# Softplus in place of bound, Exp and Ln in the first attention layer of a two-layer decoder, with a new instruction order

## The chip, the cores and the metric

The kernel runs on one core of one Trainium2 chip. The metric is device time in microseconds (us), from one launch. PE is the matmul engine, PEld its weight loads, DVE the vector engine, ACT the engine that evaluates functions and evacuates accumulators, POOL a general engine that cannot read the accumulators (PSUM), and SP issues nearly all transfers.

## The reference

2048 tokens of width 1024 get 16 meta tokens ahead of them. Two layers follow, each as norm, projection, attention, gate, output projection, residual; then a last norm.

```python
# layer 0: two groups of 8 heads
z = q @ k * 64**-0.5                              # stick-breaking heads
log_beta = log_sigmoid(z)
log_1m = where(s < t, log_beta - z, 0)            # = -softplus(z)
a = where(s < t, exp(log_beta + suffix_sum(log_1m)), 0);  o_sb = a @ v
p = softmax(where(s <= t, qk * 96**-0.5, -1e30)); o_mla = p @ v   # latent heads
h += concat(o_sb * silu(g_sb), o_mla * silu(g_mla)) @ w_out
# layer 1: 16 heads on a window of 128 keys, 16 meta keys, a sink logit, ALiBi
h += (attention(h) * silu(g)) @ w_out
out = rmsnorm(h)[:, meta dropped]
```

Since log_beta + suffix is z minus the sum of softplus over this key and all later keys, `a` is the exponential of one number for each key and query.

## The kernel before, in words

The sequence is cut into 17 blocks of 122 positions. Matmuls of the projections, of the scores and of the sums over keys take 32-bit operands that are rounded to a shorter format (`fp32r`), each split into a high and a low part, so that one product is three matmuls. The products with values (`av`, `mav`) are done in full 32 bit.

The stages, in order: norm, transposition and value projection (to about 100 us); the latent vectors and the other projections of layer 0, with the row maxima of the latent heads (to about 720 us); attention of layer 0 (to about 1645 us); output projection, norm and transposition, `out_mm`, `scale`, `turn`, `place` (to about 1865 us); the projections of layer 1; then attention of layer 1, in units of four heads of one block of 108 queries, between whose matmuls the kernel puts first the matmuls of the gates (`gates`, to about 2380 us) and then those of the last output projection (`project`, `final`, to the end).

**Layer 0 attention.** Heads go in 4 pairs, queries in 5 groups of up to 4 blocks (488 columns). For each pair and group a loop runs over key blocks. One step of the loop does, for both heads of the pair:

- `qks` (PE): scores of the stick-breaking head into `zp` (PSUM), 2 matmuls. Row 0 of each key block is an extra row that carries the running sum from key block to key block.
- `z` (DVE): `zcl` bounds the scores at 44 in place; on the diagonal it takes the minimum with a table `mz` that also holds the mask.
- `e`, `l` (ACT): `sp` = Exp of `zp`, then Ln(1 + `sp`) in place; together a softplus.
- `c` (DVE): `carry` writes row 0 of `sp` from row 0 of the step before.
- `h`, `lo`: high part (a cast, DVE) and low part (a difference, POOL, or DVE if the plan moves it) of `sp`.
- `tri` (PE): 2 matmuls with a triangle of -1 add the sums into `zp`; `a` (ACT): Exp of `zp`; `avs` (PE): product with the values.
- `qkm` (PE, 3 matmuls, a mask matmul on the diagonal), `p` (ACT: Exp), `acc` (POOL: sum of `p`), `avm` (PE) for the latent head.

At the end of a group `dn` (PE) makes the denominators, `rd` (ACT) their reciprocals as Ln and then Exp(-x), `rm` (POOL) multiplies, and `og` goes to DRAM. The values of the stick-breaking heads are stored doubled, because row 0 of the first step gives ln 2 to each sum.

The order of these instructions on each engine is fixed ahead of time: `attention_plan` lists the operations with costs and dependencies, `list_schedule` places them by a priority (`RANK`), by the sizes of the buffer rings (`RINGS`; `zp` has 2 per head) and by rules on when an operation may move to its second engine (`MOVE`). Engines then run that order and wait on semaphores.

**Functions on ACT.** ACT holds one table of functions at a time. The first instruction of the kernel loads the table `natural_log_exp_and_others`, which has Exp and Ln; Copy and Square are used with any table. Besides attention 0, Ln and Exp stand in `rstd` (L390 Ln, L391 Exp: one reciprocal root of the mean square; 17 blocks after attention 0, 16 of the last norm) and in `gate_evac` (L1662 Exp, L1663 Ln, L1664 Exp: the gate's sigmoid, 40 pieces). The softmax of layer 1 is Exp alone (L1576).

In layer 1 the units follow each other in one written order: `scores(x)` on PE and its maxima on DVE, `scale(x-1)` on DVE and POOL, filler matmuls, `trans(x-2)` on PE with its copies `ptsb` on ACT (L1598) and DVE, `exps(x)` on ACT, filler matmuls, `attend(x-3)`. A gate's three ACT operations are put in at the next filler but one after its matmuls.

Of the kernel before, what the change touches and what calls it, by code (L numbers as in the profile page):

```python
# [45 lines left out]
def constants():  # L46
# [15 lines left out]
    me = np.full((P, GW), ZMAX, f)  # L62
    me[1:BC, :BK] = np.where(i[:, None] < i[None, :], ZMAX, NEG)
    c["mz"] = me
    c["mk"], c["mk0"] = mk, mk0
# [58 lines left out]
def attention_plan():  # L124
# [31 lines left out]
    def act(n):  # L156
        return n / 1.4 + 196

    def gps(n):
        return n * 2.1 + 148  # L160

    groups = [(p, g) for p in range(NPAIR) for g in (4, 3, 2, 1, 0)]
    qk_s = qk_m = None
    q_ends, done, i = [], {}, 0
    for gi, (p, g) in enumerate(groups):
# [9 lines left out]
        for t in range(G.b1):  # L175
# [12 lines left out]
            for m in range(2):  # L188
                b_zp, b_a, b_sp, b_h, b_l = (buf(f"{x}{m}") for x in ("zp", "a", "sp", "h", "l"))
                qk_s = op("qks", s, m, "PE", pe(2, s.ns), [qk_s], [b_zp], late=late_s)  # L190
                o = op("z", s, m, "DVE", dve(s.ns) + 60, [qk_s])
                o = op("e", s, m, "ACT", act(s.ns) - 40, [o], [b_sp])
                o = op("l", s, m, "ACT", act(s.ns), [o])
                if prev:
                    o = op("c", s, m, "DVE", dve(prev.ns), [o, tri[m]], rel=[b_tri[m]])
                o = op("h", s, m, "DVE", dve(s.ns), [o], [b_h], alt=("ACT", act(s.ns)))
                o = op("lo", s, m, "Pool", gps(s.ns), [o], [b_l], [b_sp], alt=("DVE", 2 * dve(s.ns)))
                o = tri[m] = op("tri", s, m, "PE", pe(2, s.ns), [o], rel=[b_h, b_l])
                b_tri[m] = b_zp
# [38 lines left out]
RINGS = dict(zp0=2, zp1=2, a0=2, a1=2, sp0=2, sp1=2, h0=2, h1=2, l0=2, l1=2, av=1, mav=1, ms=2,  # L238
             p0=2, p1=2, acc0=3, acc1=3)
RANK = dict(qks=-8.69, z=-2.85, e=2.79, l=-3.38, c=0.83, h=6.8, lo=-5.92, tri=-1.18, a=3.58, avs=1.76, ogs=-0.44, qkm=-1.61, p=3.19, acc=8.47, avm=1.59, ogm=7.44, dn=1.64, rd=-5.97, rm=-9.39, head=0.74, other=-3.4)  # L240
MOVE = dict(lo=922, acc=1386, h=1245)
HEAD = {("lo", "tri"): -200, ("a", "avs"): -40, ("p", "avm"): -40}
CROSS = dict(PE=220, ACT=190, DVE=150, Pool=130)
OWN = dict(ACT=140, DVE=60, Pool=120, PE=0)


def list_schedule(ops, rank=RANK, move=MOVE, rings=RINGS):

    engines = ("PE", "ACT", "DVE", "Pool")
    free = dict(rings)  # L250
    users, wait, rt, pri = {}, {}, {}, {}
# [10 lines left out]
    while len(out) < len(ops):  # L262
        again = True
        while again:
            again = False
            for e in engines:
# [3 lines left out]
                for src in engines:  # L270
                    for o in ready[src]:
                        own = src == e
                        if rt[o] > now or not own and (not o.alt or o.alt[0] != e or busy[src] - now < move[o.kind]):
                            continue
                        if any(free[b.ring] <= 0 for b in o.acq):
                            continue
                        k = (pri[o][0] + (0 if own else rank["other"]), pri[o][1])
                        if best is None or k < best[0]:
                            best = (k, o, src)
                if best:  # L280
                    _, o, src = best
                    ready[src].remove(o)
                    for b in o.acq:
                        free[b.ring] -= 1
                    o.on, o.start = e, now
                    busy[e] = now + (o.cost if src == e else o.alt[1])
                    tick += 1
                    heapq.heappush(events, (busy[e], tick, "end", o))
                    out.append(o)
                    again = True  # L290
        if not events:
            break
        while True:
            now, _, what, x = heapq.heappop(events)
            if what == "end":
                for y, w in x.outs:
                    wait[y] -= 1
                    rt[y] = max(rt[y], now + w + (CROSS if y.eng != x.on else OWN)[x.on])
                    if wait[y] == 0:
# [3 lines left out]
                for b in x.rel:  # L303
                    users[b] -= 1
                    if users[b] == 0:
                        tick += 1
                        heapq.heappush(events, (now + CROSS[x.on], tick, "free", b))
# [11 lines left out]
def build(tc, a, off, upto=99):  # L319
# [121 lines left out]
    def open_b2():  # L441
# [6 lines left out]
        dma(cp, a["pack"][:, p0:p1])  # L448
        for n in ("ident", "tri", "mk", "mk0"):
# [72 lines left out]
    with ExitStack() as st:  # L522
# [20 lines left out]
        with ExitStack() as st2:  # L543
# [442 lines left out]
    with b2:  # L986
# [21 lines left out]
        def qks(s, m):  # L1008
# [5 lines left out]
            T.matmul(zp[:BC, :s.ns], k[:, 2 * m, c], q, start=True, stop=False)  # L1014
            T.matmul(zp[:BC, :s.ns], k[:, 2 * m + 1, c], q, start=False, stop=True)  # L1015

        def on_(e):
            return V if e == "DVE" else G

        def zcl(s, m):  # L1020

            z = s.zp[m][:BC, :s.ns]
            if s.bs >= s.G.b0:
                V.tensor_tensor(z, z, C("mz")[:BC, :s.ns], op=ALU.min)
            else:
                V.tensor_scalar(z, z, ZMAX, None, op0=ALU.min)  # L1026

        def exp1(s, m):
            sp = s.sp[m] = work(f"sp{m}", 2)
            S.activation(sp[:BC, :s.ns], s.zp[m][:BC, :s.ns], AF.Exp)  # L1030

        def log1(s, m):
            sp = s.sp[m][:BC, :s.ns]
            S.activation(sp, sp, AF.Ln, bias=1.0)  # L1034

        def carry(s, m):

            n, k = s.ns, s.prev.ns
            V.tensor_scalar(s.sp[m][0:1, n - k:n], s.prev.zp[m][0:1, :k], -1.0, None, op0=ALU.mult)  # L1039

# [19 lines left out]
        def aexp(s, m):  # L1060
            x = s.a[m] = work(f"a{m}", 2)
            S.activation(x[:BC, :s.ns], s.zp[m][:BC, :s.ns], AF.Exp)  # L1062

# [66 lines left out]
        def rden(s, m):  # L1130
            g, n = s.G, s.G.n
            r = g.r = work("rd", 1)
            S.activation(r[:, :n], g.dn[:, :n], AF.Ln)
            S.activation(r[:, :n], r[:, :n], AF.Exp, scale=-1.0)

        def rmul(s, m):
# [746 lines left out]
```

## Time and profile before

| | us |
|---|---|
| median of 3 runs (lowest, highest) | 2658.41 (2655.79, 2659.16) |
| the profiled execution, its own device time | 2655.23 |
| its span, first to last instruction | 2653.3 |
| PE busy in the span | 2605.3 (98%) |
| DVE, ACT, POOL busy | 1680.3, 1348.5, 1113.2 |
| layer 0 attention, 723 to 1645 us | 922 |
| gates beside layer 1 attention, 2096 to 2380 us | 284 |

Busy is the time in which an engine executes. PE's matmuls overlap, and their ends in the trace are modelled, so that a busy PE may still be one that waits; the start of one matmul to the start of the next is the safer measure. The trace's columns "idle before, releaser" say what ended an engine's wait. The profiled execution is 3.18 us below the median of the runs.

### The profile page before, as it was taken

How to read it: one execution, taken by the hardware profiler on the slowest of the kernel's cores; microseconds unless marked ns; L12 is line 12 of the kernel's file. 1: busy time of each engine (PE TensorE's matmuls, PEld its weight loads, DVE VectorE, ACT ScalarE, POOL GpSimd, SP SyncE). 2: the span in 40 equal slices, each digit the busy share in tenths (PEclk: the TensorE clock that was granted, in tenths of full speed). 3: DMA queues.
4: the chain of work that ended last, by engine and by line, in shares of the span. 5: the costliest groups of instructions: out<-in, count | busy, mean ns of one | idle time of the engine just before them, and what ended most of it. 6: DMA issues, size and time to landing. Idle time of an engine off the chain costs nothing.

```text
span 2653.3 us, 39563 instructions
## 1 busy us (share of the span) xinstructions
PE 2605.3 (98%) x13241; PEld 1961.4 (74%) x13241; DVE 1680.3 (63%) x3699; ACT 1348.5 (51%) x3311; POOL 1113.2 (42%) x938
## 2 busy tenths in 40 slices
PE   9999999999989999999999999999999999999998
PEld 7888888998945555555555555788999988777776
DVE  5366486777267767767776776433322478897884
ACT  6542121212267777777777776332222477764442
POOL 1012210010078878878877887410000123446552
PEclk9999999999999999999999999999999999999999
DMA  5476634342593351252232112643644545677652
GB/s 148 105 217 175 187 105 117 87 113 75 149 188 82 77 147 50 66 130 48 69 86 77 35 35 75 187 121 92 164 115 123 129 122 138 160 185 220 180 169 98
DMA packets 337862, 321.53 MB, mean 121 GB/s; under 512 B 143670, under 2 KB 319610, under 8 KB 337075
## 3 DMA queue, kind: packets, MB, share of 16 engines
q1 hardware_dynamic: 336939, 318.12, 44.9%
q8 instruction: 104, 1.70, 0.3%
q14 instruction: 99, 0.81, 0.1%
q10 hardware_dynamic: 720, 0.89, 0.1%
HBM read 198.46 MB, written 120.80 MB: 120 GB/s over the span
## 4 chain that ended last, share of the span: by engine, by line
PE 88%; DVE 4%; DMA 2%; ACT 2%; issue 1%; SPq 1%; POOL 1%; DVEq 0%; POOLq 0%; ACTq 0%
PE psd L397 8%; PE psd L398 8%; PE psd L399 8%; PE pso L1758 7%; PE psg L1645 6%; PE mav L1116 5%; PE av L1070 5%; PE zp L1014 4%; PE zp L1057 3%; PE psx L934 3%; PE zp L1058 3%; PE zp L1015 2%; PE pso L1238 2%; PE pso L1236 2%; PE pso L1237 2%; PE ms L1090 2%
## 5 line engine op out<-in xcount | busy, mean ns | idle before, releaser
L1052 POOL TENSOR_TENSOR l<-sp,h 123x488 fp32r<-123x488 f32 (+3 forms) x347 | 373.1, 1075 | 159.2 <-DVE h L1047 80.4
L1585 POOL TENSOR_TENSOR s_sb<-s_sb,den 108x1008 f32<-108x1008 f32 (+1 forms) x76 | 151.6, 1995 | 513.5 <-DVE den L1584 459.7
L1108 POOL TENSOR_TENSOR acc<-acc,p 122x488 f32<-122x488 f32 (+3 forms) x288 | 309.7, 1085 | 14.6 <-ACT p L1098 13.3
L397 PE MATMUL psd<-xh,wh 128*128 128x366 f32 (+1 forms) x760 | 274.3, 361 | 0.0
L399 PE MATMUL psd<-xh,wl 128*128 128x366 f32 (+1 forms) x760 | 267.9, 352 | 0.0
L398 PE MATMUL psd<-xl,wh 128*128 128x366 f32 (+1 forms) x760 | 267.7, 352 | 0.0
L1047 DVE CAST h<-sp 123x488 fp32r<-123x488 f32 (+2 forms) x360 | 243.4, 676 | 18.2 <-ACT sp L1034 8.2
L1030 ACT ACTIVATE sp<-zp 123x488 f32<-123x488 f32 (+2 forms) x360 | 184.5, 515 | 94.9 <-DVE zp L1026 55.7
L1039 DVE TENSOR_SCALAR sp<-zp 1x488 f32<-1x488 f32 (+3 forms) x320 | 183.1, 572 | 74.2 <-ACT a L1062 59.3
L1062 ACT ACTIVATE a<-zp 123x488 f32<-123x488 f32 (+2 forms) x360 | 184.6, 517 | 85.5 <-PE zp L1058 51.7
L1034 ACT ACTIVATE sp<-sp 123x488 f32<-123x488 f32 (+2 forms) x360 | 197.3, 551 | 6.3
L1026 DVE TENSOR_SCALAR zp<-zp 123x488 f32<-123x488 f32 x224 | 150.0, 669 | 74.0 <-PE zp L1015 68.8
L1014 PEld LDWEIGHTS zp<-q,kbig 128*123 128x123 f32 x320 | 58.8, 184 | 158.6 <-DVE sp L1039 90.4
L1098 ACT ACTIVATE p<-ms 122x488 f32<-122x488 f32 (+3 forms) x320 | 156.3, 513 | 35.1 <-PE mav L1116 21.7
L1576 ACT ACTIVATE s_sb<-s_sb,nm 108x252 f32<-108x252 f32 (+1 forms) x304 | 149.4, 495 | 31.5 <-DVE nm L1567 31.3
L398 PEld LDWEIGHTS psd<-xl,wh 128*128 128x128 f32 x760 | 144.1, 190 | 15.8 <-issue 0.9
L397 PEld LDWEIGHTS psd<-xh,wh 128*128 128x128 f32 x760 | 144.0, 189 | 12.6 <-issue 0.7
L1116 PE MATMUL mav<-p,mvbig 122*64 122x488 f32 (+3 forms) x640 | 147.4, 539 | 5.4 <-DMA mvbig<-d_mv 5.4
L399 PEld LDWEIGHTS psd<-xh,wl 128*128 128x128 f32 x760 | 143.5, 189 | 10.9
L1070 PE MATMUL av<-a,vbig 123*64 123x488 f32 (+3 forms) x640 | 145.4, 532 | 0.0
L387 POOL TENSOR_TENSOR wl<-raw,wh 128x1024 fp32r<-128x1024 f32 x17 | 40.8, 2401 | 245.5 <-DVE wh L386 159.1
L1014 PE MATMUL zp<-q,kbig 128*123 128x488 f32 (+3 forms) x320 | 136.1, 428 | 7.3 <-DVE sp L1039 4.6
(514 smaller groups left out, 6825.6 us busy)
## 6 DMA issues: line engine op xcount, KB each, us to landing
kbig<-d_sk SPq DMA_DIRECT2D x32, 492.0 KB
q<-d_q SPq DMA_DIRECT2D x36, 432.0 KB
xt<-in_x SPq DMA_DIRECT2D x32, 448.0 KB
raw<-in_od_w_in SPq DMA_DIRECT2D x48, 256.0 KB
mq<-d_mq SPq DMA_DIRECT2D x32, 373.6 KB
raw<-in_ev_w_in SPq DMA_DIRECT2D x19, 512.0 KB
kkb<-d_kk SPq DMA_DIRECT2D x18, 472.0 KB
xt<-d_h SPq DMA_DIRECT2D x16, 512.0 KB
```

The source lines that it names most:

```text
L397: T.matmul(o, wh[:, k, m0:m1], xh[:, k, c0:c1], start=(k == 0), stop=False)
L398: T.matmul(o, wh[:, k, m0:m1], xl[:, k, c0:c1], start=False, stop=False)
L399: T.matmul(o, wl[:, k, m0:m1], xh[:, k, c0:c1], start=False, stop=(k == k_n - 1))
L1014: T.matmul(zp[:BC, :s.ns], k[:, 2 * m, c], q, start=True, stop=False)
L1034: S.activation(sp, sp, AF.Ln, bias=1.0)
L1047: V.tensor_copy(h[:BC, :n], sp[:BC, :n])
L1052: on_(on).tensor_tensor(l[:BC, :n], s.sp[m][:BC, :n], f(s.h[m][:BC, :n]), op=ALU.subtract)
L1062: S.activation(x[:BC, :s.ns], s.zp[m][:BC, :s.ns], AF.Exp)
L1070: T.matmul(s.G.av[64 * m:64 * m + 64, s.js:s.G.n], v[:BC, bi, 64 * m:64 * m + 64], s.a[m][:BC, :s.ns], start=s.first, stop=s.last, skip_gr ...
L1108: eng.tensor_tensor(g.acc[m][:BK, s.jm:g.n], g.acc[m][:BK, s.jm:g.n], s.pt[m][:BK, :n], op=ALU.add)
L1116: T.matmul(s.G.mav[64 * m:64 * m + 64, s.jm:s.G.n], v[:BK, bi, 64 * m:64 * m + 64], s.pt[m][:BK, :s.nm], start=s.first, stop=s.last)
L1758: T.matmul(ps, l[:, k], r[:, k, c], start=(k == 0 and x == 0), stop=(k == KT - 1 and x == 2))
```

## The change

- The scores get no bound. On a diagonal block one more matmul (122 columns, identity times a mask table `ms`) adds the mask into `zp`. `z` is gone from DVE.
- `e` and `l` become one ACT operation, Softplus of `zp`.
- `a` becomes Softplus too: the extra row now holds 32 times what it held, so that all sums are lower by 32 ln 2, where softplus and Exp are the same number; the values are scaled by 2^32 instead of 2. `carry` divides by 32.
- `p` becomes Softplus: the latent scores get a constant of -384 (-39.2 after the scale) through a constant row of the keys; the denominators take it out again.
- `rd` becomes a Copy of the denominators, and `recip` (new, `rc`) takes the reciprocals on DVE in pieces of 122 columns, 68 in all.
- The planner gets other costs, latencies by pair of engines, other priorities and a rule for rings in which a buffer is taken in order; the order of attention 0 on all four engines is new.

```diff
-    te[:BC, 0] = te[0] = -1
+    te[:BC, 0] = -1
+    te[0] = -CW
...
+    crow[1, 0::2] = -MOFF
...
-RANK = dict(qks=-8.69, z=-2.85, e=2.79, l=-3.38, ...)
-MOVE = dict(lo=922, acc=1386, h=1245)
+RANK = dict(qks=-5.12, e=6.78, rc=-14.5, c=-8.79, ...)
+MOVE = dict(lo=685, acc=2297, h=121)
...
-                S.activation(vt[:BK], pss.pop(b)[:BK], AF.Copy, scale=2.0)
+                S.activation(vt[:BK], pss.pop(b)[:BK], AF.Copy, scale=2.0 ** CW)
...
-            T.matmul(zp[:BC, :s.ns], k[:, 2 * m + 1, c], q, start=False, stop=True)
+            T.matmul(zp[:BC, :s.ns], k[:, 2 * m + 1, c], q, start=False, stop=(s.bs < s.G.b0))
+            if s.bs >= s.G.b0:
+                T.matmul(zp[:BC, :BK], rnd["ident"][:BC, :BC], rnd["ms"][:BC], start=False, stop=True)
...
-            S.activation(sp[:BC, :s.ns], s.zp[m][:BC, :s.ns], AF.Exp)
-        def log1(s, m):
-            sp = s.sp[m][:BC, :s.ns]
-            S.activation(sp, sp, AF.Ln, bias=1.0)
+            S.activation(sp[:BC, :s.ns], s.zp[m][:BC, :s.ns], AF.Softplus)
...
-            S.activation(x[:BC, :s.ns], s.zp[m][:BC, :s.ns], AF.Exp)
+            S.activation(x[:BC, :s.ns], s.zp[m][:BC, :s.ns], AF.Softplus)
...
-            S.activation(pt[:BK, :s.nm], s.ms[m][:BK, :s.nm], AF.Exp, scale=MSC)
+            S.activation(pt[:BK, :s.nm], s.ms[m][:BK, :s.nm], AF.Softplus, scale=MSC)
...
-            S.activation(r[:, :n], g.dn[:, :n], AF.Ln)
-            S.activation(r[:, :n], r[:, :n], AF.Exp, scale=-1.0)
+            S.activation(r[:, :n], g.dn[:, :n], AF.Copy)
+        def recip(s, m):
+            r = s.G.r[:, m * BK:(m + 1) * BK]
+            V.reciprocal(r, r)
```

The built order of the engines shows what the diff alone does not. In attention 0 as a whole, ACT loses 360 Ln and gets 146 of the casts `h`; DVE loses 360 bounds and 146 casts and gets 110 of POOL's differences `lo` (123 instead of 13) and 68 reciprocals; POOL keeps 237 of 347 `lo`. PE gets 136 mask matmuls; it changes from a rounded matmul to a full 32-bit one and back 303 times, where it did so 332 times before.

DVE in the middle of a long group of attention 0, before (L1026 the bound, L1039 the carry of a head, L1047 the cast):

```order
L1026 TENSOR_SCALAR zp_10672<-zp_10672 123x488
L1039 TENSOR_SCALAR sp_10667<-zp_10593 1x488
L1047 CAST h_10694<-sp_10667 123x488
L1026 TENSOR_SCALAR zp_10696<-zp_10696 123x488
L1039 TENSOR_SCALAR sp_10691<-zp_10617 1x488
L1047 CAST h_10719<-sp_10691 123x488
L1026 TENSOR_SCALAR zp_10721<-zp_10721 123x488
```

The same place in the changed kernel (L1036 the carry, L1044 the cast, L1049 the difference):

```order
L1036 TENSOR_SCALAR sp_9405<-zp_9358 1x488
L1036 TENSOR_SCALAR sp_9381<-zp_9322 1x488
L1044 CAST h_9428<-sp_9381 123x488
L1049 TENSOR_TENSOR l_9443<-sp_9381,h_9428 123x488
L1036 TENSOR_SCALAR sp_9449<-zp_9398 1x488
L1036 TENSOR_SCALAR sp_9439<-zp_9372 1x488
L1044 CAST h_9474<-sp_9439 123x488
L1049 TENSOR_TENSOR l_9489<-sp_9439,h_9474 123x488
```

For one step of two heads DVE had two bounds, two carries and two casts; now it has two carries, one cast and one difference. The other head's cast stands on ACT and its difference on POOL.

ACT beside layer 1 attention, before: the gate's Exp, Ln, Exp, then the copy of transposed probabilities and the next unit's Exp (`s_sb`).

```order
L1662 ACTIVATE sl_20074<-sl_20074 128x356
L1663 ACTIVATE sl_20074<-sl_20074 128x356
L1664 ACTIVATE sl_20074<-sl_20074 128x356
L1598 ACTIVATE ptsb<-pt 128x432
L1576 ACTIVATE s_sb,den<-s_sb,nm 108x252 x4
L1578 ACTIVATE se<-se 108x4
L1662 ACTIVATE sl_20135<-sl_20135 128x356
```

The same place in the changed kernel, whose source there is the same:

```order
L1662 ACTIVATE sl_19540<-sl_19540 128x356
L1663 ACT_TABLE_LOAD
L1663 ACTIVATE sl_19540<-sl_19540 128x356
L1664 ACT_TABLE_LOAD
L1664 ACTIVATE sl_19540<-sl_19540 128x356
L1598 ACTIVATE ptsb<-pt 128x432
L1576 ACTIVATE s_sb,den<-s_sb,nm 108x252 x4
L1578 ACTIVATE se<-se 108x4
```

A table load now stands ahead of each Ln and of each Exp that follows a Ln. The built program has 148 of them, where it had 1: one at the start, one at the first Softplus, 80 in the 40 gate pieces, 34 in the 17 `rstd` of the output projection of layer 0, and 32 in the 16 `rstd` of the last norm. Inside attention 0 there is none beyond the first.

ACT at the very end, before (L1777 the squares, L390 and L391 the root, L1786 half of the output, L1788 its transfer):

```order
L1777 ACTIVATE yt,ss_26429<-xt 128x512 x2
L390 ACTIVATE ss<-ss,epst 128x1
L391 ACTIVATE ss<-ss 128x1
L1786 ACTIVATE yt<-spare,ss 128x512
L1788 DMA out<-yt 128x512
```

The end of the changed kernel (`rstd` now has the lines L395 and L396):

```order
L1777 ACTIVATE yt,ss_25895<-xt 128x512 x2
L395 ACT_TABLE_LOAD
L395 ACTIVATE ss<-ss,epst 128x1
L396 ACT_TABLE_LOAD
L396 ACTIVATE ss<-ss 128x1
L1786 ACTIVATE yt<-spare,ss 128x512
L1788 DMA out<-yt 128x512
```

The two loads stand between the last squares and the last output.

More of the change, by code (lines that the diff above doesn't have):

```diff
@@ L58, in constants @@
     te = np.zeros((P, BC), f)
-    te[:BC, 0] = te[0] = -1
+    te[:BC, 0] = -1
+    te[0] = -CW
     te[1:BC, 1:] = -(i[:, None] >= i[None, :]).astype(f)
     c["tri"] = te
-    me = np.full((P, GW), ZMAX, f)
-    me[1:BC, :BK] = np.where(i[:, None] < i[None, :], ZMAX, NEG)
-    c["mz"] = me
+    ms = np.zeros((P, BK), f)
+    ms[1:BC] = np.where(i[:, None] < i[None, :], 0, NEG)
+    c["ms"] = ms
     c["mk"], c["mk0"] = mk, mk0
@@ L203, in attention_plan @@
             if s.last:
-                done[p, g] = [op("ogs", s, 0, "DVE", dve(G.n), [o], rel=[b_av])]
+                b_og = buf("og")
+                done[p, g] = [op("ogs", s, 0, "DVE", dve(G.n), [o], [b_og], [b_av, b_og], late=gdone[-2] if gi > 1 else ())]
             pp, bp = [], []
@@ L214, in attention_plan @@
                 else:
-                    o = op("acc", s, m, "Pool", gps(s.nm), [x, acc[m]], rel=[b_p], alt=("DVE", 1.8 * dve(s.nm)))
+                    o = op("acc", s, m, "Pool", gps(s.nm), [x, acc[m]], rel=[b_p], alt=("DVE", 2.2 * dve(s.nm)))
                     acc[m] = o
@@ L222, in attention_plan @@
             if s.last:
-                og = op("ogm", s, 0, "DVE", dve(G.n), [o], rel=[b_mav])
-                b_dn = buf("ms")
+                b_dn, b_og, b_rd = buf("ms"), buf("og"), buf("rd")
+                og = op("ogm", s, 0, "DVE", dve(G.n), [o], [b_og], [b_mav], late=gdone[-2] if gi > 1 else ())
                 o = op("dn", s, 0, "PE", pair(G.n), acc, [b_dn], b_acc)
-                o = op("rd", s, 0, "ACT", 2 * act(G.n), [o], rel=[b_dn])
-                done[p, g].append(op("rm", s, 0, "Pool", gps(G.n), [o, og]))
+                o = op("rd", s, 0, "ACT", act(G.n), [o], [b_rd], [b_dn])
+                for m in range(G.b1 - G.b0):
+                    o = op("rc", s, m, "DVE", 8 * dve(BK) - 400, [o])
+                done[p, g].append(op("rm", s, 0, "Pool", gps(G.n), [o, og], rel=[b_og, b_rd]))
+                gdone.append(done[p, g])
             prev = s
@@ L238 @@
 RINGS = dict(zp0=2, zp1=2, a0=2, a1=2, sp0=2, sp1=2, h0=2, h1=2, l0=2, l1=2, av=1, mav=1, ms=2,
-             p0=2, p1=2, acc0=3, acc1=3)
-RANK = dict(qks=-8.69, z=-2.85, e=2.79, l=-3.38, c=0.83, h=6.8, lo=-5.92, tri=-1.18, a=3.58, avs=1.76, ogs=-0.44, qkm=-1.61, p=3.19, acc=8.47, avm=1.59, ogm=7.44, dn=1.64, rd=-5.97, rm=-9.39, head=0.74, other=-3.4)
-MOVE = dict(lo=922, acc=1386, h=1245)
+             p0=2, p1=2, acc0=3, acc1=3, og=2, rd=1)
+RANK = dict(qks=-5.12, e=6.78, rc=-14.5, c=-8.79, h=30.95, lo=-11.62, tri=-1.69, a=7.61, avs=5.01, ogs=13.94, qkm=-3.42, p=5.87, acc=-21.83, avm=2.63, ogm=15.74, dn=1.3, rd=-0.65, rm=-0.05, head=1.03, other=-4.61)
+MOVE = dict(lo=685, acc=2297, h=121)
 HEAD = {("lo", "tri"): -200, ("a", "avs"): -40, ("p", "avm"): -40}
-CROSS = dict(PE=220, ACT=190, DVE=150, Pool=130)
-OWN = dict(ACT=140, DVE=60, Pool=120, PE=0)
+LAT = {("PE", "PE"): 0, ("PE", "ACT"): 200, ("PE", "DVE"): 200, ("PE", "Pool"): 250, ("ACT", "ACT"): 95,
+       ("ACT", "PE"): 250, ("ACT", "DVE"): 200, ("ACT", "Pool"): 195, ("DVE", "DVE"): 60, ("DVE", "PE"): 320,
+       ("DVE", "ACT"): 180, ("DVE", "Pool"): 230, ("Pool", "Pool"): 60, ("Pool", "PE"): 80, ("Pool", "DVE"): 80,
+       ("Pool", "ACT"): 80}
 def list_schedule(ops, rank=RANK, move=MOVE, rings=RINGS):
     engines = ("PE", "ACT", "DVE", "Pool")
-    free = dict(rings)
+    held = {r: [] for r in rings}
     users, wait, rt, pri = {}, {}, {}, {}
@@ L274, in list_schedule @@
                             continue
-                        if any(free[b.ring] <= 0 for b in o.acq):
+                        if any(len(held[b.ring]) >= rings[b.ring] and users[held[b.ring][-rings[b.ring]]] for b in o.acq):
                             continue
@@ L303, in list_schedule @@
                 for b in x.rel:
[L304 to L307, printed above, removed]
+                    tick += 1
+                    heapq.heappush(events, (now + 200, tick, "free", b))
             elif what == "free":
-                free[x.ring] += 1
+                users[x] -= 1
             if not events or events[0][0] > now:
@@ L448, in open_b2 @@
         dma(cp, a["pack"][:, p0:p1])
-        for n in ("ident", "tri", "mk", "mk0"):
+        for n in ("ident", "tri", "ms", "mk", "mk0"):
             src = ident if n == "ident" else C(n)
@@ L1139, in rmul @@
             put(g).dma_start(d_og[g.g][:, 4 + g.p], g.og[:, :n])
-        RUN = dict(qks=qks, z=zcl, e=exp1, l=log1, c=carry, h=high, lo=low, tri=tri, a=aexp, avs=avs, ogs=ogs,
-                   qkm=qkm, p=pexp, acc=accum, avm=avm, ogm=ogm, dn=den, rd=rden, rm=rmul)
+        RUN = dict(qks=qks, e=soft, c=carry, h=high, lo=low, tri=tri, a=aexp, avs=avs, ogs=ogs,
+                   qkm=qkm, p=pexp, acc=accum, avm=avm, ogm=ogm, dn=den, rd=rden, rc=recip, rm=rmul)
         left = [2] * len(groups)
```

39 lines of the change are left out of this document (16 added, 23 removed).

## The prediction

> **What bounds the kernel now.** I read the busy shares first, then stages, then in each stage what PE waits for. Columns of the first fence: stretch, its length, busy us (instructions) of PE, PEld, DVE, ACT, POOL, granted clock, DMA share, GB/s. The stretches are attention 0, the output projection, gates beside attention 1, the rest of attention 1, the tail.
>
> ```profile
> PE 2605.3 (98%) x13241; PEld 1961.4 (74%) x13241; DVE 1680.3 (63%) x3699; ACT 1348.5 (51%) x3311; POOL 1113.2 (42%) x938
> 723.00:1645.00 922.00, 904.25 (x4179) 505.09 (x4177) 653.74 (x1092) 693.82 (x1480) 732.57 (x686) 0.99 0.33 83
> 1645.00:1865.00 220.00, 214.83 (x1001) 171.98 (x1002) 87.03 (x149) 69.51 (x155) 54.27 (x51) 0.98 0.46 138
> 2096.00:2380.00 284.00, 281.86 (x1767) 239.36 (x1765) 239.53 (x791) 206.62 (x666) 101.03 (x50) 1.00 0.57 144
> 2380.00:2610.00 230.00, 229.30 (x1282) 176.12 (x1281) 181.25 (x507) 106.10 (x381) 135.40 (x62) 1.00 0.65 190
> ```
>
> PE is the bound throughout, at full clock; ACT is idle for 77.4 us of the gates' 284 and for 123.9 of the 230 behind them.
>
> In attention 0 "busy" hides waits, so I count PE's work from the chain of waits at places where PE only follows itself (columns: start us, us to the next link):
>
> ```profile
> 739.15 12.68 DMA mkbig<-d_kr
> 1300.25 0.22 PE zp L1015
> 1300.48 0.23 PE ms L1090
> 1301.15 0.97 PE mav L1116 x4
> 1302.12 0.42 PE zp L1014
> 1302.54 0.22 PE zp L1015
> 1325.02 0.06 PE ms L1094
> ```
>
> A rounded matmul of 488 columns takes 0.223 us on average, a pair of value products (x4) 0.97, the first rounded matmul after it 0.20 more, a mask of 122 columns 0.06. The loops hold 306 full widths for each of the seven rounded matmuls of a head and 306 value pairs: 306 x 7 x 0.223 = 478; 306 x 0.97 = 297; 332 changes back x 0.20 = 66; 20 denominators (16 wide, 4 narrow) about 17; 136 masks 8. Together 866 of 922 us. The other 56 are waiting; 13 of them are the transfer at 739, which the change leaves. So 43 us can be won at most.
>
> ```profile
> PEld zp L1014 <- DVE sp L1039: 93.5, 144, 2.6
> DVE zp L1026 <- PE zp L1015: 59.4, 102, 1.4
> DVE sp L1039 <- ACT a L1062: 50.1, 94, 1.6
> ACT sp L1030 <- DVE zp L1026: 49.5, 72, 1.4
> ```
>
> Here (waits from 800 to 1600: total us, times, longest) the next scores wait for the carry L1039, which frees their PSUM buffer; the carry waits for `a`, the Exp for the bound.
>
> **The change in attention 0.** The rows of its operations (busy us, mean ns):
>
> ```profile
> L1034 ACT ACTIVATE sp<-sp 123x488 f32<-123x488 f32 (+2 forms) x360 | 197.3, 551 | 6.3
> L1030 ACT ACTIVATE sp<-zp 123x488 f32<-123x488 f32 (+2 forms) x360 | 184.5, 515 | 94.9 <-DVE zp L1026 55.7 <-DVE zp L1024 28.8 <-POOL acc L1108 6.6
> L1133 ACT ACTIVATE rd<-dn 128x488 f32<-128x488 f32 (+1 forms) x20 | 10.3, 517 | 4.5 <-PE dn L1128 2.7 <-PE av L1070 1.6
> L1134 ACT ACTIVATE rd<-rd 128x488 f32<-128x488 f32 (+1 forms) x19 | 10.7, 563 | 0.6
> L1026 DVE TENSOR_SCALAR zp<-zp 123x488 f32<-123x488 f32 x224 | 150.0, 669 | 74.0 <-PE zp L1015 68.8 <-ACT a L1062 3.9
> L1024 DVE TENSOR_TENSOR zp<-zp,cp 123x122 f32<-123x122 f32 (+3 forms) x136 | 63.1, 470 | 78.6 <-PE zp L1015 67.3 <-PE zp L1057 7.7 <-ACT sp L1034 2.7
> L1047 DVE CAST h<-sp 123x488 fp32r<-123x488 f32 (+2 forms) x360 | 243.4, 676 | 18.2 <-ACT sp L1034 8.2
> L1052 DVE TENSOR_TENSOR l<-sp,h 123x488 fp32r<-123x488 f32 (+1 forms) x13 | 19.0, 1465 | 0.4
> L1052 POOL TENSOR_TENSOR l<-sp,h 123x488 fp32r<-123x488 f32 (+3 forms) x347 | 373.1, 1075 | 159.2 <-DVE h L1047 80.4 <-PE zp L1015 15.5 <-PE zp L1057 14.6
> 2485.66 0.16 DVE L1583 TENSOR_TENSOR den<-den,se 108x4 f32<-108x4 f32 x1
> 2485.85 0.18 DVE L1584 RECIPROCAL den<-den 108x4 f32<-108x4 f32 x1
> ```
>
> No Softplus is in the trace. Out of PSUM a Ln takes 517 ns (L1133) and an Exp 515 (L1030): size and source set the time, not the function, so I take 515 for Softplus, with 551 (out of SBUF) as the far end. For the wide reciprocal the nearest row is 4 columns: 0.18 us against 0.16 for an addition of that size, some 5 ns per column more. The lower end of one piece is 0.18 us; 122 columns at 5 ns on top of a narrow operation of some 0.3 give 0.9, which I take since the width is what differs.
>
> ACT: 693.8 - 197.3 (Ln) - 10.7 + 146 casts x 0.551 = 566 us. DVE: 653.7 - 150.0 - 63.1 - 146 x 0.676 + 110 x 1.465 + 68 x 0.9 = 564. POOL: 732.6 - 110 x 1.075 = 614. The fullest engine goes from 79% of the stage to 67%, and a head's chain from scores to `a` loses a bound and a Ln, 1.2 us of work. What is late next is the carry, behind one cast and one difference of 1.5 us on DVE, less than before. PE itself: 136 masks x 0.06 = 8 us more, 29 changes fewer x 0.20 = 6 less. I take 30 of the 43 us as won, so 30 - 2 = 28. Ends: all of it won, -41; or the stalls only move behind the longer DVE operations, 0 won and as much as 10 us worse. The table load at the first Softplus lies before ACT's first wait for PE; the two value scales and the smaller constants cost nothing (same instructions); the tail of the stage changes a Ln and an Exp for a Copy and one narrow reciprocal, even.
>
> **The table loads behind attention 0.**
>
> ```profile
> L348 ACT ACT_TABLE_LOAD x1 | 1.3, 1283 | 0.7 <-PEq L1870 0.7
> 2107.98 0.49 ACT L1662 ACTIVATE sl<-sl 128x356 f32<-128x356 f32 x1
> 2108.50 0.50 ACT L1663 ACTIVATE sl<-sl 128x356 f32<-128x356 f32 x1
> 2109.04 0.50 ACT L1664 ACTIVATE sl<-sl 128x356 f32<-128x356 f32 x1
> L1598 ACT ACTIVATE ptsb<-pt 128x432 f32<-128x432 f32 x41 | 21.6, 527 | 51.1 <-PE pt L1595 50.9
> L1576 ACT ACTIVATE s_sb<-s_sb,nm 108x252 f32<-108x252 f32 x172 | 84.5, 495 | 16.2 <-DVE nm L1567 16.1
> ```
>
> Gates: 80 loads x 1.283 = 102.6 us on an ACT with 77.4 idle in that stage. Even if it never idled it would need 309 us of 284, 25 too many. Its idle time is mostly in front of `ptsb` and the Exps, whose inputs come from PE, POOL and DVE through a queue that now also waits for the gates: DVE's product with the gate and its low weight parts stand behind ACT's. I keep a fifth of the idle, 16 us: 25 + 16 = +41. Ends: +15, if PE leaves ACT a backlog of 10 us (about one and a half units) that drains in the next stage; +103, if none of the idle time can be used.
>
> The one load in the trace has no function ahead of it, so a wait for ACT to empty would not show in it. The Trainium skill (ScalarE: Activation LUTs, What ACT_TABLE_LOAD costs) gives 1283 ns for the load, as here, and some 1380 ns more for a drain, 2.66 us a switch; the gates would then need 80 x 2.66 = 213 us, an estimate by that page.
>
> Output projection: two loads lengthen each `rstd` by 2.57 us.
>
> ```profile
> 1745.09 0.20 ACT L391 ACTIVATE ss<-ss 122x1 f32<-122x1 f32 x1
> 1749.90 0.28 PE L1269 MATMUL pso<-ident,ss 122*128 122x122 f32 x1
> 2647.90 0.19 ACT L1777 ACTIVATION_READ_ACCUMULATOR yt<-xt 128x1 f32 x1
> 2648.31 0.29 ACT L390 ACTIVATE ss<-ss,epst 128x1 f32<-128x1 f32 x1 [0.23 <-DVE ss L1783]
> ```
>
> PE wants the root 4.6 us after it is there, since half a block's matmuls lie between: hidden, +0 (without that cover 17 x 2.57 = 44). The last norm: 15 x 2.57 = 38.5 us on an ACT with 123.9 idle; the next unit's Exps come later, but `trans` takes them two units on. I take +4 (0 to 38). The tail is bare: the first load starts at 2648.1 and ends 1.1 us after the Ln could have run, the second costs 1.28: +2.3.
>
> **Sum.** -28 + 41 + 0 + 4 + 2.3 = +19.3 on the profiled execution's 2655.23, which stands 3.2 below the median; on the median 2658.41 that is 2678.
>
> **The rivals.**
>
> Faster: the same sum with both disputed terms at their good ends. ACT may lag PE in the gates without stopping it, because its results are taken two units later; then the stage costs 15, attention 0 gives 41, and the last norm nothing: -41 + 15 + 2.3 = -24, 2635. It decides when PE's waiting in the gates stays under 26 us or so against a gain of 28. For it: ACT's idle stretches are spread over all units. Against: 25 us is the floor of ACT's own time there. I also count here that the loads cost nothing, 2630; the 1.28 us row speaks against it.
>
> Emptied ACT: if a load waits until ACT is empty and the next function until the load is through, with about twice the row's time, the gates' ACT needs 206.6 + 205 = 412 us for 284. That is +128 with no idle at all, +133 with little; the roots of the output projection are then 5.1 us late against 4.6 of cover, some 10 us in all; the last norm about +10, the tail +5. With -28 it comes to 2788. The Trainium skill (ScalarE: Activation LUTs, What ACT_TABLE_LOAD costs) has this rule. Against it: each of the loads stands behind a short function of some 0.5 us, and no drain is written in the built order.
>
> Level: attention 0 wins 36 or more and the gates lose 36, 2658.
>
> **Chances.** Forecast 0.60, with a range of its own from 2664 to 2730; faster 0.16; emptied ACT 0.13; level 0.11. A change under 0.2%, 5 us, is about what a measurement of this kernel cannot tell from none. So faster 0.16, same 0.11, slower 0.73. The range 2643 to 2735 leaves out the emptied ACT, the best of the faster cases and a little above; its upper end is attention 0 at -28 with the gates near +95.
>
> **What would show it.** Right: attention 0 shorter by 18 to 40 us, the waits for L1039's successor mostly gone, Softplus near 515 ns; table loads in ACT's rows at 1.28 us; the gates' stage 300 to 350 us long with ACT over 90% busy and PE waiting for `pt` or the gates' buffers; the output projection as long as before. Wrong: a gates' stage under 300 us (ACT's work overlapped better than I count), functions that start over 1.5 us after a load's start plus end (emptying), or an attention 0 that keeps its 922 us because DVE's differences or reciprocals run longer than 1.5 and 0.9 us.

## The result, and the profile after

The changed kernel takes 2683.5 us (median of four runs, 2682.1 to 2684.1) against 2657.9 for the kernel before (2655.8 to 2659.2): a ratio of 1.0096, 95% interval 1.0079 to 1.0114. The profiled run has a span of 2681.6 us against 2653.3.

The first fence is from the page of the changed kernel (busy us and share of each engine); behind it the five stretches of the prediction, moved by the few us by which each stage now starts earlier or later (stretch, length, busy us and instructions of PE, PEld, DVE, ACT, POOL, granted clock, DMA share, GB/s).

```profile
PE 2614.3 (97%) x13377; PEld 1987.8 (74%) x13377; DVE 1612.0 (60%) x3372; ACT 1420.5 (53%) x3224; POOL 1014.7 (38%) x828
```

```profile
722.00:1637.00 915.00, 898.01 (x4316) 525.33 (x4315) 576.49 (x765) 586.53 (x1248) 637.42 (x577) 0.99 0.33 84
1637.00:1860.00 223.00, 216.52 (x1002) 171.89 (x1003) 85.98 (x143) 108.85 (x179) 54.48 (x50) 0.98 0.44 133
2091.00:2405.00 314.00, 291.79 (x1765) 242.08 (x1764) 230.03 (x792) 301.92 (x744) 100.35 (x50) 0.98 0.51 131
2405.00:2638.00 233.00, 233.00 (x1291) 179.35 (x1290) 199.88 (x508) 137.68 (x407) 132.22 (x62) 0.99 0.64 186
2638.00:2681.00 43.00, 34.55 (x150) 26.61 (x148) 12.99 (x17) 17.88 (x27) 0.00 (x0) 0.94 0.21 74
```

Read the ACT column. In attention 0 it fell from 694 to 587 us. In the gates' stage it rose from 207 of 284 to 302 of 314: ACT is full there, and PE has 22 us without work. DVE and POOL of attention 0 fell as worked out ahead (564 and 614 forecast, 576 and 637 measured).

The groups of the new operations and of those that moved (busy us, mean ns of one | idle before them):

```profile
L1029 ACT ACTIVATE sp<-zp 123x488 f32<-123x488 f32 (+2 forms) x360 | 177.0, 518 | 75.4 <-PE zp L1020 45.7 <-PE zp L1022 20.2 <-POOL acc L1105 4.2
L1134 DVE RECIPROCAL rd<-rd 128x122 f32<-128x122 f32 x68 | 59.0, 886 | 11.3 <-ACT rd L1130 11.1
L1044 DVE CAST h<-sp 123x488 fp32r<-123x488 f32 (+3 forms) x214 | 169.3, 794 | 11.8 <-ACT sp L1029 5.3
L1049 DVE TENSOR_TENSOR l<-sp,h 123x488 fp32r<-123x488 f32 (+3 forms) x123 | 153.9, 1254 | 16.9 <-ACT h L1042 13.6
L1663 ACT ACT_TABLE_LOAD x40 | 51.3, 1283 | 0.7
L1664 ACT ACT_TABLE_LOAD x40 | 51.3, 1283 | 0.7
L395 ACT ACT_TABLE_LOAD x33 | 42.3, 1283 | 0.6
L396 ACT ACT_TABLE_LOAD x33 | 42.3, 1283 | 0.6
```

Softplus costs 518 ns (515 forecast), the reciprocal 0.89 us (0.9), and the 146 table loads stand where the sum had put them: two for each gate, two for each `rstd`.

Since the program's order behind attention 0 is the same in all these kernels, five landmarks on PE give the length of each stage. They are the first score matmul of attention 0, its last value product, the last matmul that spreads an `rstd` (L1269), and the first and last matmul of the gates; the rest ends with the span. All times are us of the profiled run:

| kernel | attention 0 | output projection | between | gates | rest |
|---|---|---|---|---|---|
| before | 921.0 | 230.8 | 214.5 | 285.2 | 278.5 |
| changed | 912.9 | 234.6 | 214.4 | 312.0 | 285.2 |
| e1_one_table | 911.9 | 228.0 | 214.4 | 285.3 | 280.2 |
| e2_before_switching | 923.2 | 235.1 | 214.4 | 311.9 | 284.8 |
| e3_half_the_switches | 912.5 | 229.1 | 214.5 | 289.0 | 282.0 |
| e4_loads_in_order | 902.3 | 229.2 | 214.4 | 285.3 | 278.3 |
| e7_latent_keys_first | 898.5 | 229.0 | 214.4 | 285.3 | 278.6 |
| e8_four_loads_per_gate | 912.5 | 228.9 | 214.4 | 423.8 | 285.6 |
| e9_before_loads_in_order | 912.9 | 229.7 | 214.5 | 285.2 | 278.3 |

So the change won 8 us in attention 0 and lost 4, 27 and 7 in three stages whose code it doesn't touch. Of the last 7, 3.6 lie between the last gate matmul and the first of the last output projection, while ACT still works on the last gates; 2.3 are the tail, and under 1 the last norm.

Each row is one execution, and the executions of one kernel lie 2 to 13 us apart. The kernel before has medians from 2655.4 to 2657.9 in the sets of runs below, so a difference of 2 us between medians of two sets says little. Each ratio is against the runs of the kernel before in the same set.

### The profile page after: what moved, and what is told of

Its sections match the earlier page's. It is cut to its first block, busy times and chain, and to the rows that moved or that the text cites. A ratio compares the mean times of both kernels' runs of the same rounds, so it can differ in the third digit from the quotient of the medians.

```text
span 2681.6 us, 39155 instructions
## 1 busy us (share of the span) xinstructions
PE 2614.3 (97%) x13377; PEld 1987.8 (74%) x13377; DVE 1612.0 (60%) x3372; ACT 1420.5 (53%) x3224; POOL 1014.7 (38%) x828
## 5 line engine op out<-in xcount | busy, mean ns | idle before, releaser
L1036 DVE TENSOR_SCALAR sp<-zp 1x488 f32<-1x488 f32 (+3 forms) x320 | 180.7, 574 | 275.2 <-PE zp L1055 173.0
L1049 POOL TENSOR_TENSOR l<-sp,h 123x488 fp32r<-123x488 f32 (+3 forms) x237 | 273.7, 1159 | 106.8 <-ACT h L1042 58.8
L1059 ACT ACTIVATE a<-zp 123x488 f32<-123x488 f32 (+2 forms) x360 | 175.4, 515 | 127.8 <-PE av L1067 106.0
L1029 ACT ACTIVATE sp<-zp 123x488 f32<-123x488 f32 (+2 forms) x360 | 177.0, 518 | 75.4 <-PE zp L1020 45.7
L1044 DVE CAST h<-sp 123x488 fp32r<-123x488 f32 (+3 forms) x214 | 169.3, 794 | 11.8 <-ACT sp L1029 5.3
L1049 DVE TENSOR_TENSOR l<-sp,h 123x488 fp32r<-123x488 f32 (+3 forms) x123 | 153.9, 1254 | 16.9 <-ACT h L1042 13.6
L1054 PE MATMUL zp<-h,tri_r 123*123 123x488 f32 (+2 forms) x360 | 141.6, 394 | 0.0
L1565 DVE CUSTOM_DVE_ANT_0 s_sb<-pss,bt,sinks 108x252 f32<-108x252 f32 (+1 forms) x304 | 127.2, 473 | 12.3 <-PE pss L1562 4.4
```

The costliest lines, as they stand in the source:

```text
L1029: S.activation(sp[:BC, :s.ns], s.zp[m][:BC, :s.ns], AF.Softplus)
L1044: V.tensor_copy(h[:BC, :n], sp[:BC, :n])
L1049: on_(on).tensor_tensor(l[:BC, :n], s.sp[m][:BC, :n], f(s.h[m][:BC, :n]), op=ALU.subtract)
L1059: S.activation(x[:BC, :s.ns], s.zp[m][:BC, :s.ns], AF.Softplus)
```

## The experiments

**One table for Ln and Exp (e1).** Behind attention 0 the table that holds both functions is loaded once, so that the later Ln and Exp find it there.

```diff
+    mark[1] = S.preload_act_table_set("natural_log_exp_and_others"); dep(tc, mark[1], mark[0])
...
-        S.activation(h, raw, AF.Copy)
+        x = S.activation(h, raw, AF.Copy); dep(tc, x, mark[1])
```

`mark[0]` is the last Copy of denominators (`rd`) of attention 0; the two dependencies keep the load between it and the first copy of the output projection.

> The changed kernel with one table load put behind attention 0, for the table that holds Exp and Ln together, so that no switch follows (3 loads in the program instead of 148). Theory A: all that was lost behind attention 0 is these loads: output projection 5 us, gates 30, last norm 1, tail 2. Then the time is 2683.5 - 38 = 2645, and within 2642 to 2650; the gates' stage has its 284 us again and each landmark behind attention 0 stands 8 to 10 us ahead of the kernel before. Theory B: part of it is the other way in which attention 0 now ends (other buffers free, other state of the queues): 2655 to 2672, with a gates' stage that stays over 290 us.

Measured 2647.4 us, ratio to the kernel before 0.996 (0.9947 to 0.9973). The gates have their 285 us again (row e1 of the table), so theory A holds: the loads cost 36 us and turn a gain of 10 into a loss of 26. The output projection is even shorter than before by 2.8, so against e1 the loads cost 6.6 there, not 4 (5.4 to 5.7 against the changed kernels further down that have no loads there either). The Trainium skill (ScalarE: Activation LUTs, Table sets: the hidden batching unit) counts one load for a Ln with an Exp behind it, since one table has both; in the changed kernel the pair came to two loads each time (146 for 73 pairs), and to none only once that table was loaded by hand.

**The loads alone (e2).** The same place in the kernel before, with the table of Exp alone, from which Ln and Exp begin to alternate:

```diff
+    mark[1] = S.preload_act_table_set("exp_and_others"); dep(tc, mark[1], mark[0])
```

> The kernel before, with a load of the Exp table alone behind attention 0, after which Ln and Exp switch tables as in the changed kernel (148 loads in the program); attention 0 is that of the kernel before. Theory A: the loads' cost has nothing to do with attention 0 and adds: 2657.9 + 38 = 2696, within 2690 to 2702, and by stages +5, +30, +1, +2. Theory B: in the changed kernel some of the 38 us belong to the way attention 0 ends: +20 to +30 here, 2678 to 2688.

Measured 2693.5, ratio 1.0137 (1.0122 to 1.0151): 36 us more than before. The stages lose 4.3, 26.7 and 6.3, much as in the changed kernel (3.8, 26.8 and 6.7), without any change to attention 0. Theory A.

**Half of the loads, and twice as many (e3, e8).** On top of e1, loads are put into the gates by hand: before the first Exp and before the Ln of every second gate in e3; and in e8 before each function of every gate and once behind them:

```diff
+                if extra:
+                    switch("exp_and_others")
                 chain(S.activation(g1[:, :n], g1[:, :n], AF.Exp))
+                if extra:
+                    switch("natural_log_exp_and_others")
                 chain(S.activation(g1[:, :n], g1[:, :n], AF.Ln, bias=1.0))
```

> As e1_one_table, with two table loads in every second gate: 40 loads, 51 us, in a stage whose ACT idles for 77 us. Theory A: loads cost only what doesn't fit into ACT's idle time, so nearly nothing: 0 to 8 us over e1_one_table, 2645 to 2653. Rival: each load delays something by its own length or a fixed part of it, whatever ACT's idle time; half of the 30 us of 80 loads, 15 us over e1_one_table, 2660.

> As e1_one_table, with four table loads in each gate: 160 loads, 205 us, in the gates' stage. Theory A (a load costs what ACT has no idle time for): ACT needs 206.6 + 205.3 = 412 us there, with 8 to 16 us idle 420 to 428, against 285: 135 to 143 us over e1_one_table, and some 5 more in the stage behind, 2782 to 2796. Rival: each load delays the stage by a fixed part, 30/80 us, whatever ACT's load: +60, 2707.

e3: 2651.6, ratio 0.9976 (0.9965 to 0.9987), 4.3 us over e1. e8: 2791.1, ratio 1.0503 (1.0488 to 1.0519), 144 us over e1. The gates' stage of e1, e3 and e8:

```profile
2079.00:2365.00 286.00, 284.73 (x1780) 243.18 (x1781) 237.57 (x789) 203.86 (x659) 99.85 (x50) 1.00 0.57 143
```

```profile
2082.00:2372.00 290.00, 287.17 (x1782) 243.76 (x1782) 232.47 (x790) 251.87 (x695) 99.21 (x50) 0.99 0.56 141
```

```profile
2083.00:2508.00 425.00, 336.40 (x1784) 273.32 (x1782) 223.13 (x789) 399.17 (x803) 97.77 (x50) 0.88 0.37 97
```

ACT's idle time (length less busy) goes 82, 38, 26 while the stage goes 286, 290, 425. With none, 40, 80 and 160 loads the gates last 285.3, 289.0, 312.0 and 423.8: the first 40 loads cost 0.09 us each, the next 40 cost 0.58 each, and the last 80 cost 1.40 each. The 1.40 are the load's own 1.28 and, in e8, a gap of 0.09 us (median) ahead of the function behind it. A fixed price per load is refuted; what counts is what no longer fits into ACT's idle time.

What PE waits for from 2091 to 2400 (us in total, times, longest), first in the kernel before, then in the changed kernel, then in e8:

```profile
PE psg L1645 <- DVE sl L1667: 1.3, 1, 1.3
```

```profile
PE psg L1645 <- DVE sl L1667: 12.7, 8, 2.8
```

```profile
PE psg L1645 <- DVE sl L1682: 45.9, 17, 5.8
PE pt L1595 <- ACT ptsb L1598: 19.6, 11, 4.1
```

A gate's matmuls wait for a PSUM buffer, which comes free with DVE's product (`sl`), which waits for ACT: these are the gates' buffers that the prediction named, before `pt`.

**The transfers at the start of attention 0 (e4, e7, e9).** In the changed kernel PE stalls twice there, for transfers (start, us, instruction, and in brackets the idle time with what ended it):

```profile
737.85 1.90 PE L1113 MATMUL mav<-p,mvbig 122*64 122x488 f32 x4 [4.33 <-DMA mvbig<-d_mv]
751.35 0.73 PE L1087 MATMUL ms<-mq,mkbig 98*122 98x488 f32 x1 [5.79 <-DMA mkbig<-d_kr]
```

The DMA engines were full then (a DMA share of 0.97 to 1.10 from 732 to 762), with the second group's queries ahead of keys that were wanted at once. e4 puts the loads on SP's queue in the order in which PE wants them:

```diff
+        with tc.manual_schedule(engines={E_.SP}):
             load_mv(0, 1)
             load_k(0, 3, mla=False)
-            load_k(0, 2)
+            load_k(0, 2, sb=False)
+            load_k(0, 2, mla=False)
...
             load_k(0, 0, mla=False)
-            load_k(0, 4, sb=False)
             load_qs(groups[1])
             load_qm(groups[1])
+            load_k(0, 4, sb=False)
```

> As e1_one_table, and at the start of attention 0 the queries of the second group (1.2 MB) are loaded behind the keys of the first, and the latent keys of block group 2 ahead of its other keys. PE waited there 4.3 us at 738 for mvbig and 5.8 at 751 for mkbig, both behind a full DMA. Theory A: both waits shrink by the 6 us that the queries' transfer takes at some 210 GB/s, 5 to 9 us off e1_one_table, 2636 to 2641. Rival: the transfers are full from 728 to 782 whatever their order, and the wait only moves to the next tile: within 2 us of e1_one_table.

Measured 2636.3, ratio 0.9916 (0.9902 to 0.993), 11 us under e1. e7 also puts `load_mk(0, 2)` ahead of the values of block group 3:

> As e4_loads_in_order, with the latent keys of block group 2 also ahead of the values of block group 3. PE waited 2.33 us for them at 743, and its clock was at 0.66 in the ten us that followed. Theory A: the wait and the slow clock behind it go, 3 to 5 us, 2631 to 2634. Rival: the values are late instead: within 1.5 us of e4_loads_in_order.

Measured 2630.5, ratio 0.9903 (0.9889 to 0.9918), 5.8 us under e4 (3.8 in attention 0), a little more than expected. It is the best version here, 26 us faster than the kernel before. The stretch from 742 to 752 in e4 and in e7:

```profile
742.00:752.00 10.00, 8.96 (x30) 5.36 (x31) 1.64 (x4) 3.63 (x8) 4.19 (x4) 0.66 1.09 208
```

```profile
742.00:752.00 10.00, 9.22 (x43) 5.57 (x44) 5.05 (x6) 6.25 (x13) 7.82 (x7) 1.00 1.10 207
```

The DMA share is as full in both. In e4 PE had stalled for 2.33 us, and the granted clock of the stretch is 0.66 with 30 matmuls done; in e7 it had stalled for 1.05, the clock is 1.00, and 43 are done. So the longer stall went with more lost time than its own length.

e9 gives the kernel before the order of e7:

> The kernel before, with the same order of transfers at the start of attention 0 as e7_latent_keys_first, and nothing else. PE waited there 5.4 us at 737 and 1.1 at 752, with a clock of 0.66 in between. Theory A: the start cost the kernel before about as much as the changed one, 6 to 12 us, 2646 to 2651; then what the change itself wins in attention 0, without the start, is the difference of the two attentions, 10 to 16 us. Rival: the old order asks for the latent keys later and loses little at its start: 0 to 3 us, 2654 to 2658, and the change's own gain is over 20.

Measured 2645.6, ratio 0.997 (0.996 to 0.9979): the start cost the kernel before 8.1 us of attention 0. It cost the changed one 13.4 (e1 to e7). With the start out of the way, attention 0 takes 912.9 us before and 898.5 after the change: the change's own gain is 14.4 (15.1 by the medians of e9 and e7).

**Is PE at its floor in attention 0? (e5, e6)** e5 takes work from PE alone; it leaves out the causal mask of the stick-breaking heads. e6 takes work from DVE and POOL alone; it leaves out the low part of the sums:

```diff
-            T.matmul(zp[:BC, :s.ns], k[:, 2 * m + 1, c], q, start=False, stop=(s.bs < s.G.b0))
-            if s.bs >= s.G.b0:
-                T.matmul(zp[:BC, :BK], rnd["ident"][:BC, :BC], rnd["ms"][:BC], start=False, stop=True)
+            T.matmul(zp[:BC, :s.ns], k[:, 2 * m + 1, c], q, start=False, stop=True)
```

> As e4_loads_in_order without the 136 mask matmuls of attention 0's stick-breaking scores (the causal mask is left out there); all other engines keep their work. Theory A: PE is at its floor in attention 0, so the time falls by what these matmuls cost on PE: 136 x 0.06 (the price in the prediction) to 136 x 0.11 (the distance between 122-column matmuls that follow each other in the trace) = 8 to 15 us, 2621 to 2628. Rival: PE still waits there for the chain over ACT and DVE, and the freed time only lengthens the waits: 0 to 3 us, 2633 or more.

```diff
-            l = s.l[m] = work(f"l{m}", 2, F32R)
-            on_(on).tensor_tensor(l[:BC, :n], s.sp[m][:BC, :n], f(s.h[m][:BC, :n]), op=ALU.subtract)
+            s.l[m] = s.h[m]
```

> As e4_loads_in_order without the low part of the split of Softplus (l = sp - h): the second triangular matmul takes h again, so PE does the same work, while DVE loses some 154 us and POOL more than that, and the chain from the scores to the next scores loses a step of 1.1 to 1.3 us. It leaves out the low part of the sums. Theory A: PE is at its floor: 0 to 5 us less than e4_loads_in_order, 2631 to 2637. Rival (the forecast's 28 us were there, and were eaten by the longer differences and reciprocals on DVE): 10 to 20 us less, 2616 to 2626.

e5: 2625.3, 11.0 under e4, with attention 0 at 892.6 (9.7 less): the masks cost PE 0.07 to 0.08 us each, and all of it is time. e6: 2633.9, 2.4 under e4, with attention 0 at 897.6 (4.7 less). Attention 0 of e4 and of e6 (columns as above):

```profile
726.00:1628.00 902.00, 893.66 (x4303) 522.93 (x4303) 577.58 (x765) 587.09 (x1248) 637.60 (x577) 1.00 0.34 84
```

```profile
726.00:1624.00 898.00, 891.06 (x4310) 522.50 (x4308) 394.70 (x642) 584.65 (x1249) 360.20 (x340) 1.00 0.35 85
```

DVE lost 183 us of work and POOL 277, and the stage 4.7. Both as theory A has it: what was left to win from DVE and POOL was under 5 us. ACT's work and the carry stayed as they were in e6, so it does not price those; but what PE waits for from 800 to 1600 comes to 2.2 us in all in e7.

**The order (e10) and the place of the mask (e11).** e10 gives e7 the tables `RANK` and `MOVE` of the kernel before, without the entries of the operations that are gone.

> As e7_latent_keys_first with the priorities of the kernel before (its two tables of numbers; the new reciprocal keeps its own), so the operations are the new ones in about the old order. Theory A: with PE at its floor, the shorter chain makes the gain and the order matters little: within 5 us of e7_latent_keys_first, 2628 to 2635. Rival: the gain in attention 0 comes from the order: 8 us slower or more, 2638 upwards.

Measured 2692.9, ratio 1.0139 (1.0125 to 1.0154): 62 us over e7. My theory was wrong here. PE is at its floor only in the new order; the same operations in about the old one, with the engines' shares that the old tables give, starve it. The loss is in attention 0 (968.8 us in the profiled run, 898.5 in e7). PE's first score matmul, from 800 to 1600, in e10 and in e7:

```profile
L1020 PE MATMUL zp<-q,kbig 128*123 128x488 f32 (+2 forms) x264 | 113.0, 428 | 19.5 <-DVE sp L1037 12.2 <-ACT a L1060 3.9 <-DMA q<-d_sq 3.1
```

```profile
L1020 PE MATMUL zp<-q,kbig 128*123 128x488 f32 (+3 forms) x286 | 115.2, 403 | 0.9 <-DVE sp L1037 0.7
```

In e10 PE sits idle for 19.5 us in front of it, mostly for the carry, and for 0.9 in e7. That is a third of the 62 us; the rest lies in matmuls further apart, and I have not settled it (the profiled run of e10 is 11 us above its median, with a clock of 0.94 all through, so its rows don't price it). The two tables were changed together, so what each of them contributes is open.

e11 puts e7's mask on DVE, as an addition of `C("ms")` to the scores in `soft`, and drops the mask matmuls:

> As e7_latent_keys_first, with the 136 mask matmuls replaced by an addition of the same mask on DVE, ahead of the Softplus (41 to 64 us more on a DVE that is 63% busy). Theory A: PE is the bound and DVE has room, so most of the 11 us that the mask matmuls cost come back: 6 to 11 us less, 2620 to 2625. Rival: the addition stands between scores and Softplus, with a semaphore more on each side, and the next scores come late by it: no gain or slower, 2629 to 2645.

Measured 2630.8, ratio 0.9907 (0.9894 to 0.992), the same as e7. The profiled run has 893.4 us in attention 0, 5 less, but it is 4 us under its median and that of e7 is 3 above, and the medians don't show it. The expected gain of 6 to 11 did not come; whether 1 or 2 us did, these runs can't tell.

## Why the prediction was right, and where its terms were not

**Forecast and outcome.** 2678 was forecast, 2683.5 measured, slower for the reason given: the loads that the change calls up behind attention 0. The net is closer than its terms, and that is luck: attention 0 came out 20 us worse than forecast and the output projection 4 worse, the gates 11 and the last norm 3 better, and these cancel in part. Two of the prediction's own signs were missed: attention 0 was to get shorter by 18 to 40 us, and the output projection was to stay as long as before.

**Attention 0: -28 forecast, -8.1 measured.** The operations were priced well in sum (Softplus, reciprocal, and the totals of ACT, DVE and POOL to within 4%); on DVE two errors cancel, since a difference took 1.25 us instead of 1.465 and a cast 0.79 instead of 0.676. What failed is the step "so 43 us can be won at most", of which 30 were taken, at two places.

The first is "13 of them is the transfer at 739, which the change leaves". The change doesn't leave it. In the kernel before, PE's two stalls there are these:

```profile
737.25 1.89 PE L1116 MATMUL mav<-p,mvbig 122*64 122x488 f32 x4 [5.39 <-DMA mvbig<-d_mv]
751.92 0.46 PE L1090 MATMUL ms<-mq,mkbig 98*122 98x488 f32 x1 [1.09 <-DMA mkbig<-d_kr]
```

The second stall ends at nearly the same time in both kernels (751.92 and 751.35), but PE stands there for 1.09 us before the change and for 5.79 after it: the new order brings PE to that block earlier, while the keys arrive no sooner. The start cost 8.1 us before and 13.4 after (e9, e7), so 5.3 us were lost there.

The second is the count of PE's work by proportion to the width. The 122-column matmuls, which the count put at a quarter of 0.223, do not run at that distance where they follow each other (the timeline of PE in the changed kernel):

```profile
722.55 0.27 PE L1020 MATMUL zp<-q,kbig 128*123 128x122 f32 x1
722.66 0.27 PE L1022 MATMUL zp<-ms_r,ident_r 123*123 123x122 f32 x1
722.77 0.27 PE L1019 MATMUL zp<-q,kbig 128*123 128x122 f32 x1
722.87 0.27 PE L1020 MATMUL zp<-q,kbig 128*123 128x122 f32 x1
```

They start 0.106 us apart instead of 0.056. There are 40 of that width of each of the seven rounded matmuls (the row of one of them):

```profile
L1054 PE MATMUL zp<-h,tri_r 123*123 123x122 f32 x40 | 10.4, 268 | 0.0
```

That is 7 x 40 x 0.05 = 14 us of PE's own work that the count took for waiting, an estimate, since no run measured it by itself (over all of them that stand between two rounded matmuls the distance is 0.100 on average, which makes it 12). The masks cost 10 to 11 us instead of 8. From the 14.4 us won without the start and the 9.7 for the masks, waits of 18 (with the 6 us of fewer changes of kind) to 24 us went away, and by e6 at most some 5 more are left on DVE's and POOL's account. So 18 to 29 us of waits were there to be won, not 43: apart from the start and these waits, the kernel before has 884 to 895 us of PE's own work, where the count had 866. The narrow matmuls are 12 to 14 us of what the count lacks; the rest is open.

**Gates: +41 forecast, +30.4 measured** (26.8 to the last gate matmul and 3.6 from there to the first matmul of the last output projection). The mechanism is the one forecast: ACT's time of 206.6 + 102.6 = 309 us is nearly the stage's length of 312. Between the landmarks, before and after:

```profile
2089.60:2374.80 285.20, 283.93 (x1775) 243.09 (x1776) 236.34 (x789) 202.85 (x654) 98.78 (x50) 1.00 0.56 142
2084.40:2396.40 312.00, 293.40 (x1775) 245.76 (x1776) 225.42 (x781) 293.65 (x727) 97.66 (x49) 0.98 0.51 128
```

ACT kept 18 us of idle time there, near the 16 forecast. But its work did not all have to be in the stage: with the loads the 202.85 us would have become 305, of which 294 were in it and some 12 ran past PE's last gate matmul, as the lower end of the range had it with 10.

**Output projection: 0 forecast, +4 measured, +6.6 against e1.** The step that failed is the cover: "PE wants the root 4.6 us after it is there". PE never waits for a root there. It waits for what stands behind a root's loads in ACT's queue, the split `bh` of the attention's output, and then for its low part on POOL (the changed kernel, ACT and PE):

```profile
1691.61 1.28 ACT L395 ACT_TABLE_LOAD   x1
1692.90 0.29 ACT L395 ACTIVATE ss<-ss,epst 122x1 f32<-122x1 f32 x1
1693.22 1.28 ACT L396 ACT_TABLE_LOAD   x1
1694.51 0.20 ACT L396 ACTIVATE ss<-ss 122x1 f32<-122x1 f32 x1
1694.62 1.09 ACT L1230 ACTIVATE bh<-raw 128x488 fp32r<-128x488 f32 x2
1695.27 0.50 PE L1236 MATMUL pso<-wo06h,bh 128*122 128x512 f32 x1 [1.01 <-ACT bh L1230]
1696.57 0.49 PE L1238 MATMUL pso<-wo06h,bl 128*122 128x512 f32 x1 [0.57 <-POOL bl L1231]
```

Behind the stage's first matmul PE waits 4.6 us in the changed kernel and 0.7 in e1, which has no loads there. The sum had priced the two loads by the cover of the root alone, and not by the instructions that follow in the same queue. What the other 2.7 of the 6.6 us are is open.

**Last norm and tail: +4 and +2.3 forecast, under 1 and 2.3 measured.** Right, the one hidden and the other bare.

**The rivals.** "Faster" needed 41 us in attention 0, more than there were. "Emptied ACT" would have put the functions 2.66 us behind the start of a load:

```profile
L1663 ACT ACT_TABLE_LOAD  x40: 1283/1283/1283, 2095.1 to 2403.6; - x40
L1663 ACT ACTIVATE sl<-sl x40: 499/504/615, 2096.4 to 2404.9; 128x356 f32<-128x356 f32 x16, 128x488 f32<-128x488 f32 x16, 128x360 f32<-128x360 f32 x8
```

The first load starts at 2095.1 us and its function at 2096.4, the last at 2403.6 and 2404.9: 1.3 us, the load itself. The Trainium skill (ScalarE: Activation LUTs, What ACT_TABLE_LOAD costs) has the 1283 ns right; its further 1380 for a drain show neither here nor in e8, where 80 more loads cost 1.40 us each.

## What to carry to other kernels

When a function from another table comes into one stage, count the table loads of all stages behind it, and load the table that the rest of the program shares once by hand: one instruction was worth 36 us here. Price work added to an idle engine by what no longer fits into its idle time in that stage, and add up what stands in its queue one behind the other, not instruction by instruction. Before putting a bound's missing time down to waits, read the distance of its narrow instructions from the timeline; and ask of every reordering which transfer is now wanted sooner.

## What the runs showed of the hardware that I had not expected

- A stall of PE can cost more than its length. The granted clock was 0.66 over the ten us around a stall of 2.33 us (e4), and 1.00 around one of 1.05 (e7). The version with 1.3 us less of stall was 3.8 us shorter in attention 0.
- No draining shows around a table load: 1283 ns is the mean of each of the four groups and the least and the most of the one whose spread is shown. In the changed kernel the load starts 0.02 us behind the function before it, and its function 0.01 us behind its end (medians of the timeline); behind the loads put in by hand in e8 it is 0.09.
- Rounded matmuls of 122 columns that follow each other start 0.106 us apart, not a quarter of the 0.223 of 488 columns; yet a mask of that width costs 0.07 to 0.08 on average (e5).
